# SSD decays from one set of in-block sums, spread per head by a one-hot product, and dt turned before its softplus

## The chip, the cores and the metric

The kernel runs on one core of a Trainium2 chip. The metric is the device time in microseconds (us) of one execution of the whole kernel. Smaller is better. The engines are named as in the profile: PE is TensorE's matmul, PEld its weight load, DVE is VectorE, ACT is ScalarE, POOL is GpSimd, SP issues the DMAs.

## The reference, cut to what matters

Four residual layers (pooling mixer, Mamba-2 SSD mixer, stick-breaking attention, pooling mixer), each with a SwiGLU feed-forward behind it, on 512 tokens of 1024 channels in float32. The change is in the SSD mixer, which occurs once. It has 32 heads of 64 channels in 8 groups of 4 heads, and a state of 128.

```python
dt = softplus(dt + dt_bias)            # (512, 32)
a  = -exp(a_log)                       # (32,)
da = dt * a
# within a chunk:
acum  = cumsum(da, axis=1)
decay = exp(where(causal, acum[t] - acum[s], -inf))
cb = einsum('btgn,bsgn->btsg', cc, bc)
y  = einsum('btsg,btsgh,bsghp->btghp', cb, decay, xc)              # xc = x * dt
y += einsum('btgn,bghpn,btgh->btghp', cc, state, exp(acum))
w  = exp(acum[-1] - acum)
state = state * exp(acum[-1]) + einsum('bsgn,bsgh,bsghp->bghpn', bc, w, xc)
```

## The kernel before

Activations are held transposed, channels on the 128 partitions and 512 tokens along the free axis. Every projection is done in fp32r with a split into a high and a low part, three matmuls for each 128 x 128 piece of weight (L215, L216, L217), so one output tile of 128 x 512 takes 24 matmuls. The weights come by DMA from SP (L94) two tiles ahead, and are split up to four pieces ahead by ACT (L108, high part) and DVE (L109, low part).

In the SSD mixer `SSD_STEPS` (L134) gives the order in which the work is written: `front` projects x, B, C and z of a group and runs the short convolution, `scan` does the chunked scan of a group in 4 blocks of 128 tokens, `out` projects two finished groups back. A scheduler then fixes one order of instructions for each engine, and interleaves them by what it expects to be ready. Each engine runs its own list strictly in order, so a projection matmul that stands between two scan matmuls covers a wait only if it stands ahead of the one that waits.

Ahead of the groups, dt is projected once (L438), with heads on 32 partitions, in a weight tile padded to 128 columns (`pad=True`, L91). Its softplus runs on tiles of 32 x 512 (L442 to L460); dt and da are then turned by eight transposes (L470, L471), and da is split into `dah` and `dal`.

In each scan, for each of the 4 blocks b, POOL builds two operands `r` of 128 x 512 (L583: the mask `le` times da of the four heads), PE multiplies them with a mask (`gtr`, L589) to get the sums between s and t for the four heads, and for b > 0 with ones (`onesr`, L591) to get the sums from the block's start. ACT takes the exponentials (L600 to `wd`, L595 to `ce`), DVE multiplies `wd` by the masked C·B product `cb` (L601) and `ce` by C (L596), and PE forms y from them (L607 within the block, L610 from the state). L615 makes the state's increments, and L622, L624 and L628 update the state. The other matmuls of a scan are the transposes of x (L543) and of B (L559), and C·B (L567). The PSUM tiles of a scan come from three banks: two of tag `m`, one of tag `s` (`bank`, L490).

Of the kernel before, what the change touches and what calls it, by code (L numbers as in the profile page):

```python
# [17 lines left out]
P = 128  # L18
SEQ = 512
# [25 lines left out]
def _cols():  # L45
    at = 0
    for name, n in (
        ("mix_norm", DEPTH * ND),
        ("ffn_norm", DEPTH * ND),
        ("pool_scale", N_POOL * ND),  # L50
        ("out_norm", D_INNER // P),
        ("conv_b", CONV_CH // P),
        ("conv_w", 4 * CONV_CH // P),
        ("ssd_d", D_INNER // P),
        ("q_norm", 1),
        ("k_norm", 1),
        ("dt_bias", 1),
        ("a_log", 1),
    ):
        COLS[name] = (at, n)  # L60
        at += n
    return at
# [65 lines left out]
def _steps(order, **names):  # L128
# [6 lines left out]
    "f0 s0 f1 s1 f2 s2 o1 f3 s3 f4 s4 o3 f5 s5 f6 s6 f7 s7 o5 o7",  # L135
    f="front", s="scan", o="out",
# [7 lines left out]
SSD_BUFS = dict(u=2, state=2, f=10, a=6, r=4, w=4, o=9, c=2)  # L144
# [3 lines left out]
class Trunk:  # L148
# [264 lines left out]
    def ssd(self, j, nxt):  # L413
# [3 lines left out]
        with self.phase("ssd", **SSD_BUFS) as tl:  # L417
# [16 lines left out]
            gtr = keep([P, P], F32R, "gtr")  # L434
            V.tensor_copy(gtr, gt)


            ps = self.ps("m")  # L438
            self.proj(ps)
            H = slice(0, HEADS)  # L440
            s = tl("o", (HEADS, SEQ))
            V.tensor_tensor(s, ps[H], self.rstd[H], op=ALU.mult)  # L442
            nc.scalar.activation(s, s, AF.Identity, bias=self.col("dt_bias", 0)[H])
            e = tl("o", (HEADS, SEQ))
            nc.scalar.activation(e, s, AF.Abs)
            nc.scalar.activation(e, e, AF.Exp, scale=-1.0)
            r = tl("o", (HEADS, SEQ))
            V.tensor_scalar(r, e, 2.0, None, op0=ALU.add)
            V.reciprocal(r, r)
            V.tensor_tensor(r, r, e, op=ALU.mult)  # L450
            r2 = tl("o", (HEADS, SEQ))
            V.tensor_tensor(r2, r, r, op=ALU.mult)
            q = tl("o", (HEADS, SEQ))
            V.tensor_scalar(q, r2, 1.0 / 17.0, None, op0=ALU.mult)
            for n in (15, 13, 11, 9, 7, 5, 3):
                V.scalar_tensor_tensor(q, q, 1.0 / n, r2, op0=ALU.add, op1=ALU.mult)
            V.scalar_tensor_tensor(q, q, 1.0, r, op0=ALU.add, op1=ALU.mult)
            V.tensor_scalar(s, s, 0.0, None, op0=ALU.max)
            dt_t = tl("o", (HEADS, SEQ))
            V.scalar_tensor_tensor(dt_t, q, 2.0, s, op0=ALU.mult, op1=ALU.add)  # L460
            na = keep([HEADS, 1], F32, "na")
            nc.scalar.activation(na, self.col("a_log", 0)[H], AF.Exp)
            V.tensor_scalar(na, na, -1.0, None, op0=ALU.mult)
            da_t = tl("o", (HEADS, SEQ))
            V.tensor_scalar(da_t, dt_t, na, None, op0=ALU.mult)

            pt = self.ps("m", [P, 2, NB, HEADS])
            for b in range(NB):
                bs = slice(b * P, (b + 1) * P)
                nc.tensor.transpose(pt[:, 0, b, :], dt_t[:, bs], self.ident[H, H])  # L470
                nc.tensor.transpose(pt[:, 1, b, :], da_t[:, bs], self.ident[H, H])  # L471
            dt = keep([P, NB, HEADS], F32, "dt")
            da = keep([P, NB, HEADS], F32, "da")
            V.tensor_copy(dt, pt[:, 0])
            V.tensor_copy(da, pt[:, 1])
            dah = keep([P, NB, HEADS], F32R, "dah")
            dal = keep([P, NB, HEADS], F32R, "dal")
            self.split(da, dah, dal)
            pf = self.ps("m", [P, 2, NB * HEADS])
            daf = da.rearrange("p b h -> p (b h)")  # L480
            mm(pf[:, 0], gt, daf, start=True, stop=True)
            mm(pf[:, 1], self.ones, daf, start=True, stop=True)
            fd = keep([P, NB, HEADS], F32, "fd")
            et = keep([P, NB, HEADS], F32, "et")
            nc.scalar.activation(fd.rearrange("p b h -> p (b h)"), pf[:, 0], AF.Exp)
            nc.scalar.activation(et.rearrange("p b h -> p (b h)"), pf[:, 1], AF.Exp)
            V.tensor_tensor(fd, fd, dt, op=ALU.mult)
# [21 lines left out]

            def front(g):  # L510
# [7 lines left out]
                for f in range(2):  # L518
# [3 lines left out]
                    conv(ps, D_INNER // P + f * GROUPS + g, bc[f])  # L522
                zs = []
# [7 lines left out]
                return xs, bc, zs  # L531

            def scan(g, xs, bc, zs):
                hs = slice(g * HPG, (g + 1) * HPG)
                bm, cm = bc

# [36 lines left out]
                py = [self.ps("y") for _ in range(2)]  # L573
                state = None
                shp = [P, HPG, P]
                for b in range(NB):
                    bs = slice(b * P, (b + 1) * P)
                    flat = "p h t -> p (h t)"
                    pd = bank(shp)
                    pe = bank(shp) if b else None  # L580
# [499 lines left out]
```

## Time and profile before

| | us |
|---|---|
| median of 3 runs | 2337.66 (2337.12 to 2338.24) |
| the profiled execution's own time | 2336.64 |
| its span | 2334.9 |
| PE busy in the span | 2297.3 |
| DVE, ACT, POOL busy | 1403.5, 951.9, 113.0 |
| SSD mixer, from its first matmul (426.4) to the first of the next feed-forward (898.6) | 472.2 |

The profile is of one execution. A busy PE is not PE at its peak: a matmul's row is longer than the time to the next one, since matmuls overlap; the price of a matmul in a stream is the difference of two starts. PE's granted clock is 2.4 GHz (1.00) in all stretches of the SSD mixer.

### The profile page before, as it was taken

The numbers are of one execution on the slowest core, as the hardware profiler recorded it, in microseconds if no ns is written. First come the engines' busy times: TensorE is split into PE (matmuls) and PEld (weight loads), VectorE is DVE, ScalarE is ACT, GpSimd is POOL, SyncE is SP. The second block draws the span as 40 slices with busy tenths as digits, with TensorE's granted clock in tenths as the row PEclk, the third lists the DMA queues.
The fourth block names the chain that finished last, engine by engine and source line by source line (L and its number), as shares of the span: only waits on it lengthen the run. The fifth ranks groups of instructions, "written<-read, shape, count | busy, mean of one in ns | idle before, by whom it ended". The sixth has DMA issues, their size and how long they took to land.

```text
span 2334.9 us, 26714 instructions
## 1 busy us (share of the span) xinstructions
PE 2297.3 (98%) x10784; PEld 1876.3 (80%) x10784; DVE 1403.5 (60%) x1937; ACT 951.9 (41%) x1334; POOL 113.0 (5%) x191
## 2 busy tenths in 40 slices
PE   8999999999999999999999999999999999999999
PEld 7888888877877778888888877778888888888887
DVE  8744434888787886434347778875344469534443
ACT  5522223565444555222225667763222244422221
POOL 0000000032021200000000101100000000000000
PEclk9999999999999999999999999999999999999999
DMA  4323232321212123223222212113223223323221
GB/s 162 112 93 105 91 100 65 109 73 55 91 55 91 55 74 107 91 95 104 90 91 91 75 44 64 55 55 108 91 92 107 82 92 98 108 95 104 90 97 66
DMA packets 211898, 205.41 MB, mean 88 GB/s; under 512 B 4800, under 2 KB 204608, under 8 KB 211776
## 3 DMA queue, kind: packets, MB, share of 16 engines
q1 hardware_dynamic: 211632, 203.57, 26.9%
q8 instruction: 85, 1.39, 0.2%
q14 instruction: 37, 0.30, 0.0%
q10 hardware_dynamic: 144, 0.14, 0.0%
HBM read 201.60 MB, written 2.10 MB: 87 GB/s over the span
## 4 chain that ended last, share of the span: by engine, by line
PE 89%; DVE 6%; ACT 3%; issue 1%; DMA 0%; SPq 0%; DVEq 0%; ACTq 0%
PE ps L215 27%; PE ps L216 27%; PE ps L217 27%; PE ps L852 2%; DVE w L601 1%; PE ps L784 1%; DVE w L596 1%; PE ps L806 1%; DVE wl L109 1%; PE ps L747 1%; PE ps L746 1%; PE ps L748 1%; PE ps L607 0%; DMA raw<-in_pool_in_dram 0%; PE ps L589 0%
## 5 line engine op out<-in xcount | busy, mean ns | idle before, releaser
L108 ACT CAST wh<-raw 128x1024 fp32r<-128x1024 f32 (+3 forms) x394 | 403.0, 1024 | 1092.2 <-PE ps L216 859.7
L215 PE MATMUL ps<-xh,wh 128*128 128x512 f32 x2056 | 803.7, 392 | 5.8 <-ACT xh L261 5.6
L216 PE MATMUL ps<-xl,wh 128*128 128x512 f32 x2056 | 802.9, 391 | 0.2 <-DVE xl L262 0.2
L217 PE MATMUL ps<-xh,wl 128*128 128x512 f32 x2056 | 803.0, 391 | 0.0
L109 DVE TENSOR_TENSOR wl<-raw,wh 128x1024 fp32r<-128x1024 f32 (+3 forms) x394 | 468.3, 1189 | 82.2 <-ACT wh L108 81.9
L215 PEld LDWEIGHTS ps<-xh,wh 128*128 128x128 f32 x2056 | 387.0, 188 | 86.2 <-ACT xh L261 6.5
L216 PEld LDWEIGHTS ps<-xl,wh 128*128 128x128 f32 x2056 | 386.9, 188 | 80.8 <-DVE xl L262 1.2
L217 PEld LDWEIGHTS ps<-xh,wl 128*128 128x128 f32 x2056 | 386.9, 188 | 80.6 <-issue 1.3
L215 PE MATMUL ps<-h,wh 128*128 128x512 f32 x736 | 286.4, 389 | 0.5 <-DVE x L393 0.5
L217 PE MATMUL ps<-h,wl 128*128 128x512 f32 x736 | 286.3, 389 | 0.0
L216 PE MATMUL ps<-h,wh 128*128 128x512 f32 x736 | 286.3, 389 | 0.0
L343 DVE TENSOR_TENSOR x<-ps,x 128x512 f32<-128x512 f32 x96 | 66.4, 692 | 256.6 <-PE ps L217 256.6
L336 DVE TENSOR_TENSOR g<-ps,g 128x512 f32<-128x512 f32 x88 | 60.6, 691 | 225.7 <-PE ps L217 225.7
L327 DVE TENSOR_TENSOR g<-ps,rstd 128x512 f32<-128x512 f32 x88 | 60.6, 691 | 219.9 <-PE ps L217 219.6
L215 PEld LDWEIGHTS ps<-h,wh 128*128 128x128 f32 x736 | 138.2, 188 | 29.5 <-DVE x L393 0.9
L216 PEld LDWEIGHTS ps<-h,wh 128*128 128x128 f32 x736 | 138.2, 188 | 28.8
L217 PEld LDWEIGHTS ps<-h,wl 128*128 128x128 f32 x736 | 138.2, 188 | 28.6
L215 PE MATMUL ps<-o,wh 128*128 128x512 f32 x192 | 76.7, 402 | 1.2 <-DVE x L678 1.1
L216 PE MATMUL ps<-o,wh 128*128 128x512 f32 x192 | 76.0, 396 | 0.0
L217 PE MATMUL ps<-o,wl 128*128 128x512 f32 x192 | 75.6, 395 | 0.0
L504 DVE SCALAR_TENSOR_TENSOR c<-u,par,c 128x512 f32<-128x512 f32 x96 | 71.4, 747 | 3.3 <-ACT c L499 1.9
L330 DVE TENSOR_TENSOR g<-g,rstd 128x512 f32<-128x512 f32 x88 | 60.0, 685 | 3.0 <-ACT g L329 2.9
(198 smaller groups left out, 2194.1 us busy)
## 6 DMA issues: line engine op xcount, KB each, us to landing
raw<-in_ffn_gate_dram SPq DMA_DIRECT2D x44, 1024.0 KB, 5.0
raw<-in_ffn_up_dram SPq DMA_DIRECT2D x44, 1024.0 KB, 4.9
raw<-in_ffn_down_dram SPq DMA_DIRECT2D x32, 1024.0 KB, 4.9
raw<-in_ssd_in_dram SPq DMA_DIRECT2D x16, 1024.0 KB, 5.1
raw<-in_ffn_down_dram SPq DMA_DIRECT2D x16, 768.0 KB, 4.3
raw<-in_ssd_in_dram SPq DMA_DIRECT2D x16, 512.0 KB, 4.5
raw<-in_ssd_out_dram SPq DMA_DIRECT2D x8, 1024.0 KB, 4.8
raw<-in_sb_qkv_dram SPq DMA_DIRECT2D x16, 512.0 KB, 3.6
```

Of the source, the lines that this page charges most:

```text
L108: self.nc.scalar.copy(wh, src)
L109: self.nc.vector.tensor_tensor(wl, src, wh.bitcast(F32), op=ALU.subtract)
L215: mm(out, wh, xh, start=start and i == 0, stop=False)
L216: mm(out, wh, xl, start=False, stop=False)
L217: mm(out, wl, xh, start=False, stop=stop and i == n - 1)
L327: nc.vector.tensor_tensor(g, ps, self.rstd, op=ALU.mult)
L330: nc.vector.tensor_tensor(sg, sg, self.rstd, op=ALU.mult)
L336: nc.vector.tensor_tensor(h, ps, h, op=ALU.mult)
L343: nc.vector.tensor_tensor(self.x[d], ps, self.x[d], op=ALU.add)
L504: V.scalar_tensor_tensor(c, u[:, k : k + SEQ], self.col("conv_w", k * nt + ch), c, op0=ALU.mult, op1=ALU.add,)
L596: V.tensor_tensor(ce, ce, cm[:, bs].unsqueeze(1).to_broadcast(shp), op=ALU.mult)
L852: mm(out, left, right, start=False, stop=last, skip_group_check=True)
```

## The change

- dt is still projected first. Its weight piece has 32 columns, not 128 with padding. The raw result is copied, turned by four transposes, and the reciprocal root mean square is turned by four more, so that softplus runs on 128 x 128 tiles with tokens on the partitions. `dt_bias` and `a_log` come repeated on all partitions.
- In-block running sums of da are formed once for all heads and blocks, in two forms: `ar` with heads on the partitions (four products with `le`, rows of high and of low part) and `acol` with tokens on the partitions.
- In `scan`, POOL builds one tile `sel` (one-hot columns of the four heads). For each head one matmul `sel` x `ar` (new L576) spreads that head's running sum over all partitions for all four blocks. ACT then takes `relu(acol - sum)` in four pieces of 128 x 128, one for each block since `acol` is a column for each block (new L583), the exponential of the sums (`ce`, L586, 128 x 384) and of the relu's result (`wd`, L587, 128 x 512). The eight operands `r` of a scan and the matmuls with `gtr` and `onesr` are gone.
- All states are formed ahead of y. DVE multiplies `wd` and `ce` by head (L663 of 128 x 512, L664 of 128 x 384) instead of by block. y is formed for two heads at a time (L673, L679). The tag `w`, of which `wd` and `ce` are, has 6 buffers; a scan uses 8 tiles of it.
- The z projection (`gate`) is a step of its own; in `SSD_STEPS` it stands where it stood.

```diff
-    "f0 s0 f1 s1 f2 s2 o1 f3 s3 f4 s4 o3 f5 s5 f6 s6 f7 s7 o5 o7",
+    "d0 x0 z0 s0 x1 z1 s1 x2 z2 s2 o1 x3 z3 s3 x4 z4 s4 o3 x5 z5 s5 x6 z6 s6 x7 z7 s7 o5 o7",
-SSD_BUFS = dict(u=2, state=2, f=10, a=6, r=4, w=4, o=9, c=2)
+SSD_BUFS = dict(u=2, state=3, f=11, a=6, w=6, o=8, c=2, d=5, sel=1)
...
+            def steps():
+                shp = [P, NB, HEADS]
+                ps = self.ps("n", [HEADS, SEQ])
+                self.gemm(ps, self.terms(self.xs.values(), slice(0, HEADS)))
+                raw = tl("o", (HEADS, SEQ))
+                nc.scalar.copy(raw, ps)
+                pt = self.ps("m", [P, NB, P])
+                for b in range(NB):
+                    nc.tensor.transpose(
+                        pt[:, b, :HEADS], raw[:, b * P : (b + 1) * P], self.ident[H, H]
+                    )
+                pr = self.ps("s", [P, NB, P])
+                for b in range(NB):
+                    nc.tensor.transpose(pr[:, b], self.rstd[:, b * P : (b + 1) * P], self.ident)
...
+                da = keep([P, NB, 4, HEADS], F32, "da")
...
+                pr = self.ps("m", [P, NB, P])
+                for b in range(NB):
+                    mm(pr[:, b], da[:, b].rearrange("p r h -> p (r h)"), le, start=True, stop=True)
+                L = slice(HEADS, 2 * HEADS)
+                ar = keep([P, NB, P], F32R, "ar")
+                nc.scalar.copy(ar, pr)
+                V.tensor_tensor(ar[L], pr[L], ar[L].bitcast(F32), op=ALU.subtract)
+                pf = self.ps("m", [P, 3, NB, HEADS])
+                for i, m in enumerate((gt, self.ones, le)):
+                    mm(pf[:, i], m, da[:, :, 0], start=True, stop=True)
...
+            def decay(g, sel, f):
+                out = []
+                for i in range(2 * f, 2 * f + 2):
+                    pb = bank([P, NB, P])
+                    mm(
+                        pb.rearrange("p b t -> p (b t)"), sel[:, i],
+                        ar.rearrange("p b t -> p (b t)"), start=True, stop=True,
+                    )
+                    wd, ce = tl("w", (P, NB, P)), tl("w", (P, NB - 1, P))
+                    h = g * HPG + i
+                    for b in range(NB):
+                        nc.scalar.activation(
+                            wd[:, b], pb[:, b], AF.Relu, scale=-1.0, bias=acol[:, b, h : h + 1]
+                        )
+                    nc.scalar.activation(ce, pb[:, 1:], AF.Exp)
+                    nc.scalar.activation(wd, wd, AF.Exp, scale=-1.0)
+                    out.append((wd, ce))
+                return out
...
             def scan(g, xs, bc, zs):
                 hs = slice(g * HPG, (g + 1) * HPG)
                 bm, cm = bc
+                sel = tl("sel", (P, HPG, P), F32R)
+                nc.gpsimd.tensor_copy(
+                    sel, pick[:, hs].unsqueeze(2).to_broadcast([P, HPG, P])
+                )
+                decays = [decay(g, sel, 0)]
...
-                    for i, part in enumerate((dah, dal)):
-                        rhs = tl("r", shp, F32R)
-                        nc.gpsimd.tensor_tensor(
-                            rhs, le.unsqueeze(1).to_broadcast(shp),
-                            part[:, b, hs].bitcast(F32).unsqueeze(2).to_broadcast(shp),
...
-                        r = rhs.rearrange(flat)
-                        mm(pd.rearrange(flat), gtr, r, start=i == 0, stop=i == 1)
-                        if b:
-                            mm(pe.rearrange(flat), self.onesr, r, start=i == 0, stop=i == 1)
...
+                for f in range(2):
+                    wds, ces = [], []
+                    for wd, ce in decays[f]:
+                        V.tensor_tensor(wd, wd, cb, op=ALU.mult)
                         V.tensor_tensor(
-                            ce, ce, cm[:, bs].unsqueeze(1).to_broadcast(shp), op=ALU.mult
+                            ce, ce, cm[:, P:].rearrange("p (b t) -> p b t", t=P), op=ALU.mult
                         )
...
-            add(ssd_in[j, :, c0 + GN :], ncols=P, pad=True)
+                elif step == "steps":
+                    add(ssd_in[j, :, c0 + GN :], piece=(ND, HEADS))
```

The order of the engines' lists changes too. First PE in the scan of group 0, before, from the block with b = 1 on: `ps` are PSUM tiles, `r` POOL's operands, L215 and L216 the projection of the next front, which stands between.

```order
L589 MATMUL ps_3445<-r_3447,gtr_3060 128x512
L589 MATMUL ps_3445<-r_3451,gtr_3060 128x512
L615 MATMUL ps_3469<-a_3391,a_3416 128x256
L215 MATMUL ps_3561<-xh_255_3010,wh_3243 128x512
L591 MATMUL ps_3446<-r_3447,onesr 128x512
L591 MATMUL ps_3446<-r_3451,onesr 128x512
L216 MATMUL ps_3561<-xl_255_3011,wh_3243 128x512
L607 MATMUL ps_3425<-w_3434,a_3389 64x128 x2
L607 MATMUL ps_3426<-w_3434,a_3389 64x128 x2
```

Four 512-column products stand around two of the next projection there. In the changed kernel (its own line numbers) the same scan begins on PE with two spreading products and the first transposes of x (L606):

```order
L576 MATMUL ps_3398<-ar_3155,sel_3396 128x512
L576 MATMUL ps_3408<-ar_3155,sel_3396 128x512
L606 MATMUL ps_3422<-ident,f_3200 128x128
L606 MATMUL ps_3422<-ident,f_3239 128x128
L215 MATMUL ps_3560<-xh_244_2817,wh_3250 128x512
L216 MATMUL ps_3560<-xl_244_2818,wh_3250 128x512
L217 MATMUL ps_3560<-xh_244_2817,wl_3251 128x512
L215 MATMUL ps_3560<-xh_245_2847,wh_3250 128x512
L216 MATMUL ps_3560<-xl_245_2848,wh_3250 128x512
L606 MATMUL ps_3427<-ident,f_3200 128x128
L606 MATMUL ps_3427<-ident,f_3239 128x128
```

The scan's own products moved apart: 48 projection matmuls stand within this scan now. On ACT the same place held, before, one table load and seven exponentials of 128 x 512:

```order
L600 ACT_TABLE_LOAD
L600 ACTIVATE w_3434<-ps_3427 128x512
L595 ACTIVATE w_3455<-ps_3446 128x512
L600 ACTIVATE w_3458<-ps_3445 128x512
L595 ACTIVATE w_3484<-ps_3475 128x512
L600 ACTIVATE w_3487<-ps_3474 128x512
L595 ACTIVATE w_3513<-ps_3504 128x512
L600 ACTIVATE w_3516<-ps_3503 128x512
```

Each of these seven reads one PSUM tile of four heads and one block. In the changed kernel it holds this (L583 relu, L566 the Silu of z, L624 the copy of B turned); two more heads with the same six instructions follow or are shown in part:

```order
L583 ACTIVATE w_3400<-ps_3398,acol_3164 128x128
L566 ACTIVATE f_3393<-f_3393 128x512
L583 ACTIVATE w_3400<-ps_3398,acol_3164 128x128 x3
L586 ACT_TABLE_LOAD
L586 ACTIVATE w_3401<-ps_3398 128x384
L587 ACTIVATE w_3400<-w_3400 128x512
L583 ACTIVATE w_3410<-ps_3408,acol_3164 128x128 x4
L586 ACTIVATE w_3411<-ps_3408 128x384
L587 ACTIVATE w_3410<-w_3410 128x512
L583 ACTIVATE w_3456<-ps_3454,acol_3164 128x128 x2
L624 COPY a_3445<-ps_3441 128x384
L583 ACTIVATE w_3456<-ps_3454,acol_3164 128x128 x2
```

Seven exponentials became 16 relus and 8 exponentials, and over the whole program the list of ACT holds 53 table loads where it held 45.

## Rows read from the trace of the kernel before

**Rows 1.** The page's first section: busy time, share of the span, instructions.

```profile
PE 2297.3 (98%) x10784; PEld 1876.3 (80%) x10784; DVE 1403.5 (60%) x1937; ACT 951.9 (41%) x1334; POOL 113.0 (5%) x191
```

**Rows 2.** Stretch of the SSD mixer: us, busy PE, PEld, DVE, ACT, POOL (instructions), clock, DMA.

```profile
426.40:898.60 472.20, 454.14 (x2352) 363.17 (x2351) 389.92 (x536) 250.16 (x333) 81.48 (x100) 1.00 0.23 73
```

**Rows 3.** The same view of eight stretches, one around each scan: their sum.

```profile
sum 186.00, PE 168.01 PEld 128.01 DVE 166.54 ACT 87.61 POOL 77.85; mean PE 21.00 PEld 16.00 DVE 20.82 ACT 10.95 POOL 9.73
```

**Rows 4.** PE's waits within the SSD mixer: total us, times, longest.

```profile
PE ps L607 <- DVE w L601: 16.5, 24, 1.3
PE ps L543 <- DVE f L528: 1.1, 2, 0.7
```

**Rows 5.** PE in order of time within scan 0: start, us, instruction, idle before.

```profile
480.05 0.44 PE L607 MATMUL ps<-w,a 128*64 128x128 f32 x4 [0.97 <-DVE w L601]
```

**Rows 6.** DVE in order of time, the same scan.

```profile
481.37 1.52 DVE L601 TENSOR_TENSOR w<-w,a 128x512 f32<-128x512 f32 x1
...
486.12 0.68 DVE L601 TENSOR_TENSOR w<-w,a 128x512 f32<-128x512 f32 x1
```

**Rows 7.** POOL in order of time, the same scan.

```profile
480.86 1.48 POOL L583 TENSOR_TENSOR r<-le,dal 128x512 fp32r<-128x512 f32 x1
```

**Rows 8.** PE in order of time at the start of scan 0.

```profile
470.99 0.38 PE L543 MATMUL ps<-ident,f 128*128 128x128 f32 x2
471.12 0.48 PE L217 MATMUL ps<-xh,wl 128*128 128x512 f32 x1
471.44 0.39 PE L215 MATMUL ps<-xh,wh 128*128 128x512 f32 x1
...
472.46 1.05 PE L567 MATMUL ps<-f,f 128*128 128x128 f32 x8
473.27 0.71 PE L589 MATMUL ps<-r,gtr 128*128 128x512 f32 x2
...
474.94 0.63 PE L589 MATMUL ps<-r,gtr 128*128 128x512 f32 x2
475.41 0.38 PE L615 MATMUL ps<-a,a 128*128 128x256 f32 x1
```

**Rows 9.** ACT's groups in the SSD mixer: busy us, mean ns, idle before.

```profile
L600 ACT ACTIVATE w<-ps 128x512 f32<-128x512 f32 x32 | 19.0, 594 | 0.3
...
L600 ACT ACT_TABLE_LOAD x8 | 10.3, 1283 | 0.1
...
L232 ACT ACTIVATE t<-ps,eps 128x512 f32<-128x512 f32 x9 | 6.2, 687 | 1.0 <-PE ps L247 0.5
...
L561 ACT COPY a<-ps 128x384 f32<-128x384 f32 x8 | 3.8, 480 | 9.4 <-PE ps L559 9.4
```

**Rows 10.** ACT in order of time just ahead of scan 0.

```profile
465.28 0.30 ACT L220 CAST dah<-da 128x128 fp32r<-128x128 f32 x1 [3.78 <-DVE da L475]
465.60 1.28 ACT L485 ACT_TABLE_LOAD   x1
466.89 0.28 ACT L485 ACTIVATE fd<-ps 128x128 f32<-128x128 f32 x1
467.06 0.27 ACT L486 ACTIVATE et<-ps 128x128 f32<-128x128 f32 x1
```

**Rows 11.** ACT's groups behind the SSD mixer, one of them.

```profile
L750 ACT ACTIVATE v<-ps,rcol 128x256 f32<-128x256 f32 x16 | 7.2, 471 | 8.6 <-PE ps L748 6.4 <-DVE rcol L883 2.1
```

**Rows 12.** DVE in order of time: the dt chain's first step, reciprocal and last copy.

```profile
437.38 0.68 DVE L442 TENSOR_TENSOR o<-ps,rstd 32x512 f32<-32x512 f32 x1
...
443.12 3.33 DVE L449 RECIPROCAL o<-o 32x512 f32<-32x512 f32 x1
...
464.96 0.28 DVE L475 COPY da<-ps 128x128 f32<-128x128 f32 x1
```

**Rows 13.** DVE's groups in the SSD mixer: the multiplications of `wd` and `ce`.

```profile
L601 DVE TENSOR_TENSOR w<-w,a 128x512 f32<-128x512 f32 x32 | 36.1, 1130 | 0.0
L596 DVE TENSOR_TENSOR w<-w,f 128x512 f32<-128x512 f32 x24 | 27.1, 1131 | 9.6 <-ACT w L595 9.6
```

More of the change, by code (lines that the diff above doesn't have):

```diff
@@ L134 @@
 SSD_STEPS = _steps(
-    "f0 s0 f1 s1 f2 s2 o1 f3 s3 f4 s4 o3 f5 s5 f6 s6 f7 s7 o5 o7",
-    f="front", s="scan", o="out",
+    "d0 x0 z0 s0 x1 z1 s1 x2 z2 s2 o1 x3 z3 s3 x4 z4 s4 o3 x5 z5 s5 x6 z6 s6 x7 z7 s7 o5 o7",
+    x="front", z="gate", d="steps", s="scan", o="out",
 )
@@ L477, in ssd @@
[L477 to L485, printed above, removed]
@@ L571, in scan @@
                 )
[L573 to L580, printed above, removed]
-                    for i, part in enumerate((dah, dal)):
-                        rhs = tl("r", shp, F32R)
-                        nc.gpsimd.tensor_tensor(
-                            rhs, le.unsqueeze(1).to_broadcast(shp),
-                            part[:, b, hs].bitcast(F32).unsqueeze(2).to_broadcast(shp),
+                decays.append(decay(g, sel, 1))
@@ new lines, in scan @@
+                states = [None]
+                sshp = [P, HPG, HD]
+                for b in range(NB - 1):
+                    pn = bank(sshp)
+                    mm(
+                        pn.rearrange("p h d -> p (h d)"), bt[:, b],
+                        fx[b // 2][:, b % 2].rearrange("p h d -> p (h d)"),
+                        start=True, stop=True,
+                    )
+                    new = tl("state", sshp)
+                    if b == 0:
+                        V.tensor_copy(new, pn)
+                    else:
+                        V.tensor_tensor(
+                            new, states[b], et[:, b, hs].unsqueeze(2).to_broadcast(sshp),
@@ L596, in scan @@
+                    states.append(new)
+                py = [self.ps("y") for _ in range(2)]
+                after = slice(1, NB)
+                for f in range(2):
+                    wds, ces = [], []
+                    for wd, ce in decays[f]:
+                        V.tensor_tensor(wd, wd, cb, op=ALU.mult)
                         V.tensor_tensor(
-                            ce, ce, cm[:, bs].unsqueeze(1).to_broadcast(shp), op=ALU.mult
+                            ce, ce, cm[:, P:].rearrange("p (b t) -> p b t", t=P), op=ALU.mult
@@ L598, in scan @@
                         )
-                    wd = tl("w", shp)
-                    nc.scalar.activation(wd, pd, AF.Exp)
-                    V.tensor_tensor(
-                        wd, wd, cb[:, b : b + 1, :].to_broadcast(shp), op=ALU.mult
-                    )
-                    for h in range(HPG):
-                        o = py[h // 2][(h % 2) * HD : (h % 2 + 1) * HD, bs]
-                        mm(o, xd[b // 2][:, b % 2, h, :], wd[:, h, :], start=True, stop=b == 0)
-                        if b and h % 2:
-                            for i, o in ((h - 1, even), (h, o)):
-                                mm(o, state[:, i, :], ce[:, i, :], start=False, stop=True)
-                        even = o
@@ new lines, in scan @@
+                        ces.append(ce)
+                    for b in range(NB):
+                        bs = slice(b * P, (b + 1) * P)
+                        for i in range(2):
+                            mm(
+                                py[f][i * HD : (i + 1) * HD, bs],
+                                xd[b // 2][:, b % 2, 2 * f + i, :], wds[i][:, b],
+                                start=True, stop=b == 0,
+                            )
+                        for i in range(2) if b else ():
+                            mm(
+                                py[f][i * HD : (i + 1) * HD, bs],
+                                states[b][:, 2 * f + i, :], ces[i][:, b - 1],
+                                start=False, stop=True,
+                            )
```

141 lines of the change are left out of this document (68 added, 73 removed).

## The prediction, made before the changed kernel ran

> **What bounds the kernel now.** I read the page's busy times first: PE is busy 98% of the span, DVE 60%, ACT 41% [rows 1]. So PE's list is the path nearly everywhere, and a change counts by what it takes off that list or out of its gaps. The change touches only the SSD mixer, so I read its stretch next: 472.2 us, in which PE is busy 454.1 us and idle 18.1 us [rows 2]. The eight stretches around the scans hold 186.0 us with PE busy 168.0, so practically all of that idle time (18.0 us) lies in the scans, and DVE is busy 166.5 of the 186.0 us there [rows 3]. PE's waits name the cause: 24 times, 16.5 us in all, L607 waits for DVE's `wd` product L601, and 1.1 us go to the z projection's product L528 [rows 4]. One of them is in [rows 5]. Last I looked at why DVE is late there: the same L601 takes 1.52 us while POOL is at its operand L583 (and POOL's own takes 1.48 us), but 0.68 us when POOL is quiet [rows 6, 7].
>
> **The change part by part.**
>
> *PE's list, scans.* Removed: in each of 8 scans 4 blocks x 2 products with `gtr` and 3 x 2 with `onesr`, 112 in all. Added: 4 spreading products per scan, 32 in all. All have 128 x 512 columns, and two of the old ones in a stream go from 474.94 to 475.41, 0.235 us each [rows 8]. Net 80 x 0.235 = **-18.8 us**. PE is the path, so this counts in full. Bounds: from 0.22 (0.32 from 471.12 to 471.44, less the break named next) to 0.24, so 17.6 to 19.2. Each change from small products to a 512-column one costs a break of about 0.1 us (L217 at 471.12 is followed only 0.32 later, [rows 8]). I count about 14 such breaks in scan 0 before and 13 after, so no term. The products of y, the states, the transposes and C·B are the same number as before.
>
> *PE's list, dt.* The projection keeps its 24 matmuls (512 tokens move, whatever the columns of weight). Four transposes of `raw` and four of the root mean square stand for eight before: nothing. Four products of da with `le` are new; the like of them, L567, takes 0.81 us for four (472.46 to 473.27, [rows 8]): +0.8. One more product with a mask, +0.2. Three more breaks, +0.3. Then a wait may come: dt's chain ran from 437.4 to 465.0 in DVE's list, its instructions on 32 x 512 taking 0.68 us and the reciprocal 3.33 [rows 12]. On 128 x 128 each takes about 0.28, as the copy there does, and the reciprocal a quarter, 0.8. Some 17 instructions save 0.4 each and the reciprocal 2.5, so 27.6 becomes about 18 us, and da comes at 453 to 456. PE reaches the first product of da 91 matmuls of its list after the second product of the mean square, near 453. I take 0.4 us of wait, bounds 0 and 3. Sum **+1.7 us**. DVE's relief of 9 us there gains nothing, since PE does not wait for DVE in that stretch before [rows 4]. The smaller split of dt's weights and the dropped memset lie beside the feed-forward's last products and are worth nothing either.
>
> *The waits in the scans.* POOL's eight operands per scan become one copy, so the doubling of DVE's products goes. L601 and L596 took 63.2 us in all [rows 13]; 32 products at 0.68 [rows 6] and 32 of three quarters of that take 38. Against that ACT has more to do. Per scan it had 7 exponentials at 0.59 [rows 9] and a load of 1.28 [rows 9]. Now it has 16 relus of 128 x 128, 4 exponentials of 384 columns (0.48, as the copy L561, [rows 9]), 4 of 512 columns and the load. No relu with a column as bias is in the trace. From below: two exponentials of 128 x 128 start 0.17 apart [rows 10]. From above: an activation scaled by a column, of twice as many elements, takes 0.47 [rows 11]. A column as bias makes L232 longer than L600 by 0.09 [rows 9], so I take 0.17 + 0.09, rounded to **0.27 us**. ACT's decays then cost 16 x 0.27 + 4 x 0.4 + 4 x 0.6 + 1.28 = 9.6 us per scan, where they cost 5.
>
> Whether PE waits for this I walked through for scan 0, with time 0 at its first spreading product, in the new lists' order. ACT: first relu at 0.45; the Silu of z, which waits for its own product on DVE, ends at 1.6; three relus to 2.4; the load to 3.7; `ce` to 4.1; `wd` to 4.7; second head's relus to 5.8, `ce` 6.2, `wd` 6.8; third head's and the copy of B between them, `ce` to 8.65. PE runs on projections between: it wants the bank of the first head at 4.2 (free at 4.1), the bank of the second at 6.05 (free at 6.2: **0.2**), the bank of the third at 8.55 (**0.15**), a bank that DVE frees after the masking of C·B at 9.4 (free at 9.9: **0.5**), its first `wd` at 10.4 (**0.15**), and the last state at 14.5 (DVE has it at 15.05: **0.6**). The fourth head's relus need a `w` buffer that PE frees only at 13.5; relus, exponentials and DVE's product end at 17.5, and PE comes there at 17.6, with ten projections ahead of it. The scan is done at 19.0, of which 1.65 are waits. Eight such are 13.2 us, where 17.6 were [rows 4]: **-4.4 us**. Bounds of the waits that are left: 0, and 5 us per scan (rivals).
>
> *ACT's other loads.* The list holds 8 table loads more, most where the Silu of the next front falls among the exponentials of the last output. At 1.28 each [rows 9] that is 10 us of ACT, which is busy 250 of 472 us [rows 2]; its cover is the projections between two scans, at least six tiles of 24 matmuls. I take nothing; if the cover failed, up to 10 us.
>
> *The sum.* 2336.6 - 18.8 + 1.7 - 4.4 = 2315.1 for the profiled execution. It lies 1.0 below the median of the runs, so **2316.1 us** as the runs are timed, 0.9% faster.
>
> The row on table loads is where the Trainium skill speaks against this change. ScalarE: Activation LUTs, What ACT_TABLE_LOAD costs, gives a switch of tables the load of about 1283 ns and then a drain of about 1380 ns. The trace agrees with the load and shows no drain: a load from 465.60 to 466.88 stands 0.02 us behind the copy before it and its exponential starts at 466.89 [rows 10]. By the page's 2.66 us, an estimate, ACT's eight further loads would cost 21 us of ACT instead of 10.
>
> **The rivals.**
>
> *No waits at all.* POOL's disturbance is gone, 48 projections cover a scan, and PE finds all ready: 2337.7 - 18.8 + 1.7 - 17.6 = 2303 us. Against it: in the scans DVE and ACT each have some 15 to 16 us of work beside PE's 17 to 18, each in order, and three banks tie them. Chance 0.13.
>
> *Loads held longer.* If ACT loses another 1.28 us at the scan's load, the length of one load [rows 9], the bank of the first head comes at 5.4 instead of 4.1, and PE loses about 1.2 more per scan: 2316 + 10 = 2326. The gap behind the load in [rows 10] speaks against it. The page above would give it, at 1.38 us. Chance 0.05.
>
> *The gain half eaten.* ACT's relus at 0.37 instead of 0.27 (no overlap at all between neighbours) put 0.4 us on each head: the second head's bank 0.8 later, the third's 1.2, the fourth's `wd` 1.6. PE's waits per scan go from 1.65 to about 3.7, +16.5 us: 2332.6, at the edge of no change. Chance for a time from 2333 to 2342.3: 0.10.
>
> *ACT paces the scan (slower).* If relus cost 0.47 each, the upper bound, ACT's decays take 12.8 us per scan; with the copy of B, a second load and the casts of weights that the list puts among them they near PE's own 17 us. PE then waits behind each head: 1.65 + 3.3 from the relus + 1.3 for the load, 6.2 us per scan, 50 us in all. 2337.7 - 18.8 + 1.7 + (50 - 17.6) = 2353 us. It decides from about 5 us of wait per scan on. For it: three engines nearly balanced in a scan. Against: 0.17 us between neighbours in [rows 10]. Chance 0.07.
>
> *The disturbance stays.* POOL's copy of `sel` could hold DVE as L583 did; but it is one instruction per scan where eight were, some 1 us, and is issued ahead of the products. No chance of its own.
>
> **How the numbers follow.** Forecast 2306 to 2326: 0.65. With the rivals 0.13 at 2303, 0.05 at 2326, 0.10 at 2333 to 2342 and 0.07 above. A measurement of this kernel tells about 0.2% (4.7 us) from no change. Faster by more than that (under 2333.0): 0.65 + 0.13 + 0.05 = 0.83. Within: 0.10. Slower (over 2342.3): 0.07. The range: from 2303 (the first rival) to 2332 (the third), leaving out some 0.05 below and 0.15 above.
>
> **What the changed profile would show.** Right, if the SSD mixer is near 451 us; PE has 75 fewer matmuls in its list; no product of `wd` or `ce` on DVE is near 1.5 us; PE's waits in the SSD mixer are 10 to 16 us and name banks, states and the mask of C·B, no longer the `wd` products 24 times; relus start 0.27 apart. Wrong, if PE's longest waits name ACT's relus or exponentials (then ACT paces), if relus take over 0.37 each, if the first spreading product or da's first product waits more than 3 us, or if casts of weights come late and projections wait behind the scans.

## The result, and the profile after

The changed kernel takes 2309.49 us (median of 4 runs, 2308.38 to 2309.99) against 2337.39 for the kernel before beside it (2335.94 to 2338.24): a ratio of 0.9882, 95% interval 0.9869 to 0.9894. It is 1.2% faster. The forecast was 2316.1 with a range of 2303 to 2332. The profiled execution's span is 2306.5 us at a mean granted clock of 0.999.

The busy times of the page, the stretch of the SSD mixer (426.6 to 871.4, from its first matmul to the first of the next feed-forward), and PE's waits in it, answer to [rows 1, 2, 4].

```profile
PE 2284.8 (99%) x10714; PEld 1857.9 (81%) x10714; DVE 1361.4 (59%) x1946; ACT 991.1 (43%) x1478; POOL 39.7 (2%) x134
```
```profile
426.60:871.40 444.80, 444.21 (x2282) 347.69 (x2281) 348.63 (x545) 289.30 (x476) 9.81 (x44) 1.00 0.25 76
```
```profile
PE ps L606 <- ACT w L586: 0.3, 1, 0.3
PE ps L526 <- DVE da L518: 0.2, 1, 0.2
```

The SSD mixer went from 472.2 to 444.8 us, which is 27.4 of the 28.4 us between the two spans. The rest lies behind the mixer, which the change leaves as it was: 1436.3 against 1435.1 us, and there the granted clock is 0.66 for some 10 us of the attention step before (1518 to 1528) and 0.83 after (1492 to 1502). So a difference of about 1 us between two profiles says nothing. The mixer's gain splits in two: PE's idle time there fell from 18.1 to 0.6 us (-17.5), and PE's busy time from 454.1 to 444.2 (-9.9). The forecast had the two the other way round: -4.4 for the waits, -17.1 for the list. The first experiment shows that 3.1 us of the busy time go with the waits.

DVE's group answers to [rows 6, 13]: the product with the mask now takes 0.68 us on average where its like took 1.13.

```profile
L663 DVE TENSOR_TENSOR w<-w,a 128x512 f32<-128x512 f32 x32 | 21.8, 683 | 0.1
```

ACT's groups and the start of its work in scan 0 answer to [rows 9, 10].

```profile
L583 ACT ACTIVATE w<-ps,acol 128x128 f32<-128x128 f32 x128 | 38.0, 377 | 25.9 <-PE ps L673 25.9
...
L586 ACT ACTIVATE w<-ps 128x384 f32<-128x384 f32 x32 | 16.5, 515 | 0.1
```
```profile
470.16 0.87 ACT L583 ACTIVATE w<-ps,acol 128x128 f32<-128x128 f32 x3
471.04 1.28 ACT L586 ACT_TABLE_LOAD   x1
472.34 0.49 ACT L586 ACTIVATE w<-ps 128x384 f32<-128x384 f32 x1
472.73 0.62 ACT L587 ACTIVATE w<-w 128x512 f32<-128x512 f32 x1
473.25 1.13 ACT L583 ACTIVATE w<-ps,acol 128x128 f32<-128x128 f32 x4
474.24 0.52 ACT L586 ACTIVATE w<-ps 128x384 f32<-128x384 f32 x1
```

A row's duration is not its price where neighbours overlap: the group's mean for a relu is 377 ns, but four of them start at 473.25 and the next instruction at 474.24, so one costs 0.25 us. The load ends at 472.32 and its exponential starts at 472.34.

What PE's list lost of the expected 17.1 us can be read where y's products stand among projections. Two pieces of PE's list in scan 0, in order of time:

```profile
484.72 0.39 PE L216 MATMUL ps<-xl,wh 128*128 128x512 f32 x1
485.04 0.44 PE L679 MATMUL ps<-w,state 128*64 128x128 f32 x4
485.41 0.50 PE L217 MATMUL ps<-xh,wl 128*128 128x512 f32 x1
485.75 0.39 PE L215 MATMUL ps<-xh,wh 128*128 128x512 f32 x1
...
487.59 0.39 PE L217 MATMUL ps<-xh,wl 128*128 128x512 f32 x1
487.90 0.54 PE L673 MATMUL ps<-w,a 128*64 128x128 f32 x5
...
489.16 0.48 PE L679 MATMUL ps<-w,state 128*64 128x128 f32 x3
489.58 0.50 PE L215 MATMUL ps<-xh,wh 128*128 128x512 f32 x1
489.91 0.39 PE L216 MATMUL ps<-xl,wh 128*128 128x512 f32 x1
```

One product of y stands in the trace as two rows. In the first piece a projection, four rows of y and a projection take 1.03 us (484.72 to 485.75); in the second a projection, 26 rows and a projection take 2.32 (487.59 to 489.91). A row costs about 0.054 us: in the first experiment's kernel, pieces of 8 rows measured in this way take 1.25 us, and pieces of 16 take 1.69. What is left of the two pieces, beside their rows and two projections at 0.227, is 0.36 and 0.46 us. That is the price of breaking the stream for a piece of y, more than three times what the prediction took from a break with other products. Over the SSD mixer, 24 of the 42 pieces stand alone between 512-column matmuls; they leave 0.36 to 0.65 us each, 0.48 on average, and the shortest pieces (2 rows) leave the most. No row names a wait in them, but idle times under 0.15 us are not listed, so a part of the dearer ones can be short waits.

### The profile page after: what moved, and what is told of

It is laid out like the page before. It is cut to its first block, busy times and chain, and to the rows that moved or that the text cites. A ratio compares the mean times of both kernels' runs of the same rounds, so it can differ in the third digit from the quotient of the medians.

```text
span 2306.5 us, 26600 instructions
## 1 busy us (share of the span) xinstructions
PE 2284.8 (99%) x10714; PEld 1857.9 (81%) x10714; DVE 1361.4 (59%) x1946; ACT 991.1 (43%) x1478; POOL 39.7 (2%) x134
## 4 chain that ended last, share of the span: by engine, by line
PE 91%; DVE 4%; ACT 3%; DMA 1%; issue 1%; DVEq 0%; ACTq 0%
PE ps L215 28%; PE ps L217 27%; PE ps L216 27%; PE ps L910 2%; PE ps L842 1%; PE ps L673 1%; PE ps L864 1%; PE ps L679 1%; DMA raw<-in_pool_in_dram 1%; ACT wh L108 1%; DVE wl L109 1%; PE ps L642 0%; PE ps L805 0%; PE ps L806 0%; PE ps L804 0%
## 5 line engine op out<-in xcount | busy, mean ns | idle before, releaser
L215 PE MATMUL ps<-xh,wh 128*128 128x512 f32 x2056 | 803.9, 392 | 6.4 <-ACT xh L261 5.9
L216 PE MATMUL ps<-xl,wh 128*128 128x512 f32 x2056 | 803.0, 391 | 0.3 <-DVE xl L262 0.3
L215 PEld LDWEIGHTS ps<-xh,wh 128*128 128x128 f32 x2056 | 385.8, 188 | 89.3 <-ACT xh L261 6.2
L216 PEld LDWEIGHTS ps<-xl,wh 128*128 128x128 f32 x2056 | 385.7, 188 | 82.0 <-DVE xl L262 1.9
L215 PE MATMUL ps<-h,wh 128*128 128x512 f32 x736 | 286.4, 389 | 0.9 <-DVE x L393 0.9
L216 PE MATMUL ps<-h,wh 128*128 128x512 f32 x736 | 286.3, 389 | 0.0
L215 PEld LDWEIGHTS ps<-h,wh 128*128 128x128 f32 x736 | 138.2, 188 | 29.7 <-DVE x L393 1.3
L216 PEld LDWEIGHTS ps<-h,wh 128*128 128x128 f32 x736 | 138.2, 188 | 28.8
L215 PE MATMUL ps<-o,wh 128*128 128x512 f32 x192 | 77.2, 405 | 1.2 <-DVE x L736 1.1
L216 PE MATMUL ps<-o,wh 128*128 128x512 f32 x192 | 77.5, 404 | 0.0
```

Source lines behind the costliest of these rows:

```text
L215: mm(out, wh, xh, start=start and i == 0, stop=False)
L216: mm(out, wh, xl, start=False, stop=False)
```

## The experiments

The theory after the first comparison: PE's waits went because POOL no longer disturbs DVE, PE is now busy all the time, and its list gave back a good part of the removed products in more and dearer breaks. The rivals: the new order with its cover took the waits away, not POOL; a product is worth less on the path than its 0.235 us; ACT is on the edge of pacing the scan. Every ratio is against the kernel before, timed beside that run on the same chip. In the diffs, "before" and "after" say which kernel was edited.

**POOL's operands made once (before).**

```diff
-                        rhs = tl("r", shp, F32R)
-                        nc.gpsimd.tensor_tensor(
+                        if (b % 2, i) not in made:
+                            made[b % 2, i] = tl(f"r{b % 2}{i}", shp, F32R)
+                            nc.gpsimd.tensor_tensor(
...
+                        rhs = made[b % 2, i]
```

> The kernel before, with GpSimd's operands made once (four tiles, used again by every scan) instead of eight per scan; the decays of the other groups and blocks are left out, every product of PE, ACT and DVE stays. Theory 1, the disturbance made the waits: DVE's products of wd and ce fall from 1.13 us to about 0.68, most of PE's 17.6 us of waits in the SSD mixer go, and the time falls from 2337.4 to 2320 to 2324. Rival, the new order (more projections between the decays and y) took the waits away: with the old order at least 12 us of waits stay, 2332 or more.

Measured: 2317.86 against 2335.91, ratio 0.9922 (0.9909 to 0.9936), 18.05 us less. The products of DVE and PE's waits in the SSD mixer:

```profile
L604 DVE TENSOR_TENSOR w<-w,a 128x512 f32<-128x512 f32 x32 | 21.9, 684 | 0.0
L599 DVE TENSOR_TENSOR w<-w,f 128x512 f32<-128x512 f32 x24 | 16.6, 692 | 19.4 <-ACT w L598 19.4
```
```profile
PE ps L544 <- DVE f L529: 1.9, 2, 1.6
```

All 24 waits for `wd` are gone in the old order of steps, with the old number of products. Theory 1 holds (the time is 2 us below its range) and the rival falls: no new order was needed for the waits. Nor was it that POOL's operands came earlier: none of PE's waits before names one of them [rows 4]. The Trainium skill says why, in SBUF — State Buffer, Who interferes with whom: a DVE instruction with two inputs in SBUF contends with a GpSimd instruction that reads SBUF. The trace agrees: 684 ns here, 1130 before. The stretch of the SSD mixer answers to [rows 2]:

```profile
428.10:881.10 453.00, 451.07 (x2351) 363.72 (x2350) 358.03 (x536) 250.06 (x332) 9.08 (x40) 1.00 0.24 76
```

PE's idle time fell from 18.1 to 1.9 us, and its busy time from 454.1 to 451.1 with the same products: most of it in matmuls that stand just ahead of a product that waited, so a wait cost a little more than the idle time that is listed for it.

**Eight POOL products put back (after).** Behind the mask of C·B in each scan, eight times over into the dead B tile:

```diff
+                for _ in range(8):
+                    nc.gpsimd.tensor_tensor(
+                        bm.rearrange("p (b t) -> p b t", t=P), cb,
+                        le.unsqueeze(1).to_broadcast([P, NB, P]), op=ALU.mult,
+                    )
```

> The changed kernel, with eight products of 128 x 512 put back on GpSimd in each scan, behind the mask of C.B (they write into the dead B tile). Theory 1, the disturbance made the waits: DVE's products of wd and ce go back to 1.1 to 1.5 us, PE's waits in the SSD mixer go from 0.6 to 8 us or more, 2317 to 2326. Rival, the cover by projections is what counts: the DVE products are slow again, but PE finds projections ahead of them and waits under 3 us, 2309 to 2313.

Measured: 2356.5, ratio 1.0088 (1.0074 to 1.0102): slower than the kernel before, and far above what theory 1 gave. PE's longest waits in the SSD mixer, DVE's groups, and three stretches of scan 0 (us, busy PE, PEld, DVE, ACT, POOL, then the granted clock, DMA share, GB/s):

```profile
PE ps L679 <- DVE w L669: 23.7, 23, 2.1
PE ps L685 <- DVE state L661: 6.1, 6, 1.6
PE ps L648 <- DVE state L661: 1.8, 1, 1.8
```
```profile
L669 DVE TENSOR_TENSOR w<-w,a 128x512 f32<-128x512 f32 x32 | 43.0, 1346 | 0.1
...
L657 DVE TENSOR_TENSOR state<-state,et 128x256 f32<-128x256 f32 x16 | 23.2, 1452 | 0.0
...
L661 DVE TENSOR_TENSOR state<-state,ps 128x256 f32<-128x256 f32 x16 | 6.5, 408 | 0.1
```
```profile
481.00:484.00 3.00, 1.47 (x15) 0.98 (x15) 3.00 (x3) 0.00 (x0) 2.84 (x3) 1.00 0.00 0
484.00:487.00 3.00, 2.90 (x13) 1.65 (x14) 3.00 (x4) 0.13 (x1) 2.84 (x3) 0.55 0.02 5
487.00:490.00 3.00, 2.34 (x11) 1.49 (x12) 3.00 (x4) 2.98 (x7) 2.92 (x2) 0.88 0.00 0
```

One of the waits in PE's order of time:

```profile
484.10 0.54 PE L679 MATMUL ps<-w,a 128*64 128x128 f32 x2 [1.63 <-DVE w L669]
```

The disturbance brings the waits for `wd` back (23 of them) and adds waits for the states, whose product with `et` goes from 0.42 us to 1.45; the cover by projections does not hold against it. The state's addition, which reads one operand from PSUM (L661), takes 0.41 us as in the changed kernel, though POOL was busy beside 14 of the 16: of these instructions, only those with both operands in SBUF got slower. The dose is larger than before's: POOL is busy 13.2 us in this scan, and one of its inputs is a full tile where before both were small tiles read over and over. And the waits cost twice here. Behind the stretch in which PE is busy 1.47 of 3 us, the granted clock is 0.55, near the lower level of 1.2 GHz. Of the 44.8 us between the spans of this run (2351.3) and of the changed kernel, 13.8 are PE busy for longer (2298.6 against 2284.8 on the page) with the same list; the waits account for the rest. In the SSD mixer of the kernel before, 24 waits of up to 1.3 us left the clock at 1.00 [rows 2, 4].

**Each spreading product twice (after).**

```diff
-                    mm(
-                        pb.rearrange("p b t -> p (b t)"), sel[:, i],
-                        ar.rearrange("p b t -> p (b t)"), start=True, stop=True,
-                    )
+                    for _ in range(2):
+                        mm(
+                            pb.rearrange("p b t -> p (b t)"), sel[:, i],
+                            ar.rearrange("p b t -> p (b t)"), start=True, stop=True,
+                        )
```

> The changed kernel with each of the 32 spreading products issued twice. Theory 1, PE is the path and a product of 512 columns costs its stream: 32 x 0.235 = 7.5 us more, 2317.0. Rival, such a product is worth less on the path (the list got only about 10 us shorter for 80 products, 0.12 each): 4 us more, 2313.5.

Measured: 2316.86, ratio 0.9916 (0.9903 to 0.993). Against 0.9881 for the changed kernel (below) that is 0.35%, 8 us, or 0.26 for each of 32 products; the spans of the two profiles differ by 7.4 us (2313.9 against 2306.5), 0.23 each. PE's waits stay at 0.4 us. A product on this list counts in full, so its price is not where the missing part of the list's gain went.

**Half of the products left out (before, with POOL's operands made once).** The same point from the other side, with its mark timed beside it; the low part of da's sums is left out.

```diff
-                    for i, part in enumerate((dah, dal)):
+                    for i, part in enumerate((dah,)):
```

> The kernel before with GpSimd's operands made once, again, as the mark for the next one: 2317.9 by the first measurement.

> The same, and the second of each pair of products (those with the low part dal) left out: 56 products of 128 x 512 less on PE, in the old order of steps; PE has no waits to speak of there. Theory, each product counts with its stream of 0.235 us: 13.2 us less, 2304.7. Rival, a removed product is worth only what the whole change showed (9.9 us of busy time for 80 products, 0.12 each): 7 us less, 2311.

Measured: the mark 2317.43, ratio 0.9912 (0.9899 to 0.9926); without the low parts 2304.57, ratio 0.9858 (0.9843 to 0.9873). 12.86 us for 56 products, 0.230 each. In the old order, where a removed product leaves the rest of the list as it was, it is worth its stream. The rival (0.12 each) falls here too.

**The dt part alone (before).** dt is projected into 32 columns and turned ahead of the softplus as in the change (with its small tiles, for one `o` buffer less); the running sums are not formed.

```diff
-            ps = self.ps("m")
-            self.proj(ps)
-            s = tl("o", (HEADS, SEQ))
...
+            ps = self.ps("n", [HEADS, SEQ])
+            self.gemm(ps, self.terms(self.xs.values(), slice(0, HEADS)))
+            raw = tl("o", (HEADS, SEQ))
+            nc.scalar.copy(raw, ps)
+            pt = self.ps("m", [P, NB, P])
...
+            s = small()
```

> The kernel before with the dt part alone changed: projected with heads on partitions and turned ahead of the softplus, no four products of da with le. DVE's 27.6 us chain becomes about 18. Theory, PE does not wait for DVE in that stretch, so nothing is won: 2337 within 2 us. Rival, the shorter chain is a part of the gain of the whole change: 2330 to 2334.

Measured: 2335.29 against 2337.64, ratio 0.9990 (0.9981 to 0.9999): 2.35 us faster, just inside the theory's range. The waits of PE in the SSD mixer have one row left:

```profile
PE ps L621 <- DVE w L615: 16.6, 24, 1.3
```

The 1.1 us that PE waited for z's product [rows 4] are gone; 0.75 of them stood at the start of scan 0 (469.79), right behind dt's chain. In the profiles the SSD mixer is 1.3 us shorter (470.9 against 472.2), 1.0 of it idle time. That much can be put down to the shorter chain; the rest of the 2.35 us can't, since behind the mixer, where both kernels do the same, the two profiles differ by as much again (1435.1 against 1436.3, with the granted clock at 0.83 and 0.66 from 1518 to 1528). The prediction had put the wait for z among those of the scans and called DVE's relief worth nothing.

**Twice the relus, all and half (after).** ACT's margin, in two doses.

```diff
-                    for b in range(NB):
+                    for b in (0, 0, 1, 1, 2, 2, 3, 3):
```
```diff
-                    for b in range(NB):
+                    for b in (0, 0, 1, 1, 2, 3):
```

> The changed kernel with each relu issued twice: 16 more per scan, about 4.2 us of ACT in each. Theory 1, ACT lies under cover: PE's idle time in the SSD mixer stays under 8 us, 2310 to 2317. Rival, ACT is close to pacing the scan: most of the 4.2 us per scan come out as waits, 25 to 34 us, 2335 to 2343.

> The changed kernel with two of the four relus of each head issued twice: eight more per scan, about 2.1 us of ACT in each, with its list holding about as many table loads (51 for 53). Theory, there is cover left on ACT for that: 2309.5 to 2313. Rival, ACT is close to pacing the scan already, as twice all relus suggests: a good part of 17 us comes out, 2318 or more.

Measured: 2313.62 with half of them twice, ratio 0.9904 (0.9887 to 0.992), just over its theory's range; 2356.27 with all twice, ratio 1.0085 (1.0072 to 1.0099), above both forecasts. The half dose costs under 5 us of the 17 that it adds to ACT, and the full one 47. In the half dose's profile PE is idle 1.7 us longer in the SSD mixer, where one wait of 2.2 us for an operand of the output projection (L706) stands, and 1.8 us are the lower clock right behind that wait: nine matmuls from 854.07 to 857.93 take 3.86 us, where nine at 0.23 take 2.07. The full dose is no clean one: the scheduler reordered ACT's list around the added work, and it now loads tables 20 times for L586 instead of 8. PE's four largest sums of waits in the SSD mixer, two of ACT's groups, and two stretches with such waits, with the clock:

```profile
PE ps L246 <- ACT t L220: 5.9, 2, 3.6
PE ps L215 <- DVE t L236: 5.3, 4, 3.1
PE ps L642 <- ACT w L586: 5.1, 1, 5.1
PE ps L215 <- ACT o L706: 5.0, 1, 5.0
```
```profile
L583 ACT ACTIVATE w<-ps,acol 128x128 f32<-128x128 f32 x256 | 83.9, 366 | 18.0 <-PE ps L673 11.9 <-PE ps L679 2.4 <-PE ps L576 1.1
...
L586 ACT ACT_TABLE_LOAD x20 | 25.7, 1283 | 0.3
```
```profile
555.00:560.00 5.00, 2.72 (x16) 2.00 (x18) 1.63 (x3) 2.66 (x5) 0.00 (x0) 0.50 0.00 0
560.00:565.00 5.00, 2.61 (x22) 1.97 (x18) 4.20 (x7) 4.68 (x13) 0.00 (x0) 0.76 0.00 0
```

The rival "ACT paces" does not hold for the kernel as it is: of about 2 us more of ACT per scan most is still covered, and no wait names the scan's relus or exponentials. It holds from somewhere between 2 and some 7.5 us more per scan (4.2 of relus, and 12 loads of 1.28 over 8 scans and 9 more elsewhere), in the order that the scheduler made of it, and then the fall is steep: L642 alone waits 5.1 us for a bank till the late exponential L586 has read it, and the lower clock (0.50 to 0.76) comes on top.

**Buffers, and y by block (after).** Two versions of the changed kernel and a mark: `wd` and `ce` with four buffers each, and on top of that y formed by block over all four heads.

```diff
-SSD_BUFS = dict(u=2, state=3, f=11, a=6, w=6, o=8, c=2, d=5, sel=1)
+SSD_BUFS = dict(u=2, state=3, f=10, a=6, wd=4, ce=4, o=8, c=2, d=5, sel=1)
...
-                    wd, ce = tl("w", (P, NB, P)), tl("w", (P, NB - 1, P))
+                    wd, ce = tl("wd", (P, NB, P)), tl("ce", (P, NB - 1, P))
```
```diff
+                heads = decays[0] + decays[1]
...
+                for b in range(NB):
+                    bs = slice(b * P, (b + 1) * P)
+                    for f, i in itertools.product(range(2), range(2)):
+                        mm(
+                            py[f][i * HD : (i + 1) * HD, bs],
+                            xd[b // 2][:, b % 2, 2 * f + i, :], heads[2 * f + i][0][:, b],
...
+                    for f, i in itertools.product(range(2), range(2)) if b else ():
```

> The changed kernel itself, as the mark for the other three of this group: 2309.5 by the first measurement, within 1.5 us of it.

> The changed kernel with four buffers each for wd and ce instead of six for both, so that the fourth head's decays wait for no product of y (one f buffer less pays for it). PE waits 0.6 us in the SSD mixer, so there is next to nothing left to win from waits. PE's list returns to a projection from something else 198 times instead of 211. Theory, each such return costs 0.1 us: 1.3 us less. Rival, returns cost nothing: no change.

> The same buffers, and y formed by block over all four heads as in the kernel before (four products with x, then four with the state) instead of two heads at a time. Theory, the list gave back 4.1 us in y's products (74.7 ns each where 64.2 and 67.1 were) because they alternate in twos: 4 us less than the kernel with the buffers alone. Rival, the pitch of the y products comes from where they stand among projections, or waiting for all four heads brings PE's waits back: no change, or up to 5 us more.

Measured: the mark 2308.85, ratio 0.9881 (0.9866 to 0.9896); the buffers alone 2310.04, ratio 0.9886 (0.9871 to 0.9901); with y by block 2305.82, ratio 0.9868 (0.9854 to 0.9883). The last is the fastest version here that computes all of the layer, 3.0 us (0.13%) under the changed kernel. The runs of these two do not overlap (2305.33 to 2306.83 and 2308.45 to 2309.23), but the intervals of their ratios do. PE's waits in the SSD mixer and the step to the next feed-forward, first the buffers alone, then with y by block:

```profile
PE ps L215 <- DVE x L736: 1.6, 1, 1.6
PE ps L215 <- ACT wh L108: 0.7, 1, 0.7
PE ps L215 <- DVE t L236: 0.4, 2, 0.2
PE ps L526 <- DVE da L518: 0.2, 1, 0.2
```
```profile
PE ps L606 <- ACT f L461: 0.4, 1, 0.4
PE ps L606 <- ACT ce L586: 0.2, 1, 0.2
PE ps L526 <- DVE da L518: 0.2, 1, 0.2
```

The expected 4 us between these two came (4.2), but not for the reason given. In the profiles the SSD mixer takes 446.1 us with the buffers alone and 442.2 with y by block. 2.1 us of that are waits of the former (2.9 against 0.8), which name the residual and a split weight and not y. The pitch of y's rows, from start to next start, went from 72.1 to 73.5 ns (256 rows with x) and from 70.2 to 68.4 (192 with the state): 0 us in sum. Another 1.6 us are the lower clock behind the longest of those waits, which ends at 579.25: nine matmuls from 579.82 to 583.47 take 3.65 us, where nine at 0.23 take 2.07.

```profile
580.00:583.00 3.00, 3.00 (x8) 2.32 (x8) 1.53 (x2) 2.60 (x5) 0.00 (x0) 0.50 0.68 239
```

Theory and measurement agree in the number by chance. The theory for the buffers (1.3 us less) can't be read from their time, 1.2 us more than the mark, since waits and clock hide it. But without the 1.6 us of clock PE is busy some 2.6 us less than in the changed kernel (443.2 - 1.6 against 444.2), and with y by block 2.9 less (441.3). Both lists hold 36 pieces of y where the changed kernel's holds 42, and six at 0.48 are 2.9 us.

## Why the prediction was right

Right: the sign, the range, and the mechanism for each of the two gains. By its steps:

- **The waits in the scans** (-4.4) were mis-sized: PE's idle time fell by 17.5 us, and with the 3.1 us of busy time that went in the first experiment the waits were worth about 20. The cause that the prediction named, POOL beside DVE, is shown by that experiment, where 18 us went with every product of the other engines kept. What failed is the walk of scan 0, which left 1.65 us of waits per scan (its five waits add up to 1.6). Its clock for PE ran too fast. With time 0 at the first spreading product (468.45), PE wants the bank behind the mask of C·B at 9.86 in the trace (478.31), just after DVE is done with it (9.81), where the walk had PE there at 9.4; it wants the last state at 16.6 (485.04), and DVE has it at 15.2, where the walk had PE there at 14.5; the scan's last product of y ends its piece at 21.1 (489.58), with no wait, where the walk had 19.0 with waits. The walk priced breaks at 0.1 us, and pieces of y cost 0.36 and more: that fits the 2 us at the last state. For the 0.2 to 0.5 us by which PE is later ahead of the first piece of y, no row names a cause. The rival "no waits at all" (0.13) was right on the waits.
- **PE's list in the scans** (-18.8) was right in price: 0.230 to 0.26 per product in two experiments. The step that failed is "about 14 breaks before and 13 after, so no term", counted in scan 0 alone. Over the SSD mixer the instruction lists hold 32 pieces of y before and 42 after, and 7 more returns to the stream from other small products. The pieces got dearer too: those that stand alone between 512-column matmuls leave 0.39 us on average in the first experiment's kernel, which has the old order and hardly a wait, and 0.48 in the changed one. At these prices, and 0.1 for the other returns, that is +8.4 us, an estimate, since only 25 and 24 of the pieces stand alone. The spreading products stand singly and take 0.262 from start to next start, +0.9. And the stream of projections itself runs slower (below), +2.4. With dt's +1.2 the sum is -5.9. To compare with it is the busy time against the first experiment's kernel, 451.1 to 444.2: -6.9, since the other 3.1 of the -9.9 went with POOL's instructions. Why the pieces got dearer stays open.
- **dt** (+1.7): the added products took what was said (four with `le` 0.97 us, three with masks 0.59 instead of 0.36, from start to next start) and da's wait was 0.2 instead of 0.4. But the shorter chain also took most of a wait of 1.1 us away.
- **ACT**: relus at 0.25 for 0.27, `ce` of head 0 from 3.9 to 4.4 on the walk's clock (3.7 to 4.1 foretold), no drain behind the load. The further table loads were under cover, as priced. "ACT paces" needed more work than there is; "loads held longer" had no trace.
- "75 fewer matmuls" shows as 70: each product of da stands in the trace as two rows.
- "The gain half eaten" and a change that does nothing had no part in it.

So two errors met in one sum: the waits were worth some 16 us more than forecast (20.6 for 4.4) and the list some 10 less (6.9 for 17.1), and that 2316 came out nearer than either is luck. The forecast of 0.65 for 2306 to 2326 held, with a sum whose two main terms should have been weighed the other way.

**What stays open.** Why the stream of projections runs slower. In the changed kernel its matmuls start 0.227 or 0.233 us apart in runs of many, at a granted clock of 1.00. The end of the SSD mixer in the changed kernel, and the same place in the kernel before with POOL's operands made once:

```profile
868.12 0.39 PE L216 MATMUL ps<-o,wh 128*128 128x512 f32 x1
...
870.92 0.39 PE L216 MATMUL ps<-o,wh 128*128 128x512 f32 x1
```
```profile
877.95 0.39 PE L216 MATMUL ps<-o,wh 128*128 128x512 f32 x1
...
880.66 0.39 PE L216 MATMUL ps<-o,wh 128*128 128x512 f32 x1
```

Twelve matmuls take 2.80 us in the one (868.12 to 870.92) and 2.71 in the other (877.95 to 880.66). Summed over the SSD mixer, the pitches between projections that follow another projection exceed 226.7 ns by 0.7 us in the kernel before and 3.2 in the changed one; its second profile shows 3.1, so it belongs to the kernel and is no chance. The runs narrow it down: every version of the kernel before, that with the dt part alone too, shows 0.7 to 0.8, and every version of the changed kernel 2.6 to 3.3, those with other buffers and with y by block too (stretches at the lower clock left out). No experiment here aimed at it. The price of a piece of y is read from rows; the two versions with six pieces less agree with it, but it was not tried by itself.

## What to carry to other kernels

Where a wait names DVE, look first at what else runs beside the product it waits for: moving eight POOL instructions per scan away was worth 18 us, as much as the streams of the 80 matmuls that the change is about, and more than what the list gave back of them left. When PE is the path, price a removed product by its stream, but count the breaks of the stream over the whole stretch and by kind, since a list cut into more pieces gives part of it back. And a walk through engines that sums work too low invents waits: check its clock against a stretch that the trace already shows.

## What the runs showed of the hardware that was not expected

- A piece of matmuls of 128 x 64 weights among 512-column ones costs 0.36 to 0.65 us beside its rows, 0.48 on average in the changed kernel; the prediction had read 0.1 for other small products [rows 8].
- Beside POOL's products, a DVE product with both operands in SBUF took 1.45 us instead of 0.42 (128 x 256), and an addition of the same size with one operand in PSUM stayed at 0.41.
- Waits on PE can cost twice. Behind waits of 1.6 us and more the granted clock fell to its lower level in four of these runs; a matmul of the stream took 0.43 us there instead of 0.23. That was worth 1.6 us of PE's time in one place, and most of 13.8 in the run with POOL's products put back. The length of one wait does not decide it. With 24 waits of up to 1.3 us in the SSD mixer before, and with one of 1.6 us in the first experiment, the clock stayed at 1.00; in the attention step of the kernel before it fell behind waits of 0.3 to 1.0 us that came close together, here in its stretches:

```profile
1513.00:1518.00 5.00, 3.08 (x12) 1.76 (x12) 4.92 (x9) 3.51 (x7) 3.08 (x4) 1.00 0.00 0
1518.00:1528.00 10.00, 7.95 (x31) 5.85 (x30) 7.26 (x15) 6.17 (x12) 0.00 (x0) 0.66 0.00 0
```

- ACT's margin ends in a cliff: 8 more relus per scan cost 5 us, 16 more (with the table loads that the new order brought) 47.
